# A two-layer trunk: waiting products queued behind dense ones, first slots as whole float32 products, rotary tables later

## The chip, the cores and the metric

One core of a Trainium2 chip runs the whole kernel in one launch. The metric is device microseconds (us) of one execution: the median of three runs is 1169.4 us, the runs lie between 1166.58 and 1169.9 us.

## The reference

```python
for l in range(2):
    shift, scale, gate = split(silu(c) @ ada_w[l] + ada_b[l])
    h = rms_norm(x, norm_pre[l]) * (1 + scale) + shift
    p = h @ w_in[l]                       # all branches' inputs, 1024 wide
    o_mla  = attention(...) ; o_rwkv = rwkv7(...) ; o_gla = gla(...)
    merged = sigmoid(gate_a) * o_mla + sigmoid(gate_b) * o_rwkv + sigmoid(gate_c) * o_gla
    x = x + gate * rms_norm(merged @ w_out[l], norm_post[l])
```

There are 256 tokens (T) of 1024 channels (D) in float32. The attention branch (MLA) compresses queries and keys, turns a part of them by a rotary table of cosines and sines of the positions, and attends in causal blocks. The RWKV-7 branch has 16 heads and a recurrent state with a delta rule. The gated linear attention (GLA) has 4 heads.

## The kernel before

Activations stand with channels on the 128 partitions and the 256 tokens along the free axis. Weights come in slots of 256 columns: two chunks of 512 KB, loaded through the SP queue into a ring of four buffers `wr` (`weights`, L336). For each chunk ScalarE (ACT) casts a rounded part `hi` (L347), and VectorE (DVE) or GpSimd (POOL) subtracts it to get the rest `lo` (L348). `split` (L385) cuts the activations in the same way into `hhi` and `hlo`. A dense slot is `dense_pair` (L376): for each of two output blocks and eight depth blocks three fp32r products, hi by hi, hi by lo and lo by hi, 48 of 128x256 in all, issued by `dense` (L360) or, token-major, by `dense_tok` (L369).

The program goes through each layer like this: a prenorm with the lora slot, the GLA gates (`gla_gates`), `rw_prep` and `rw_chain` for the first half of the RWKV heads, `gla`, then `rw_prep` and `rw_chain` for the second half, `mla` with the RWKV output as filler, and `finish`. For layer 0 the prenorm is `start` (L271): it loads the input transposed (`xn`, 1 MB), takes the norm through `sums`, `rms_row`, `to_rows` and `spread`, and works six slots (lora, two rk, two rr, one rv) depth block by depth block, since the modulation of each depth block comes from two 512 KB chunks of `ada_w` (`ada_part`, L257; DVE multiplies and accumulates each at L266).

`rw_chain` (L556) first forms Gram matrices, sends the small triangular systems through DRAM (tiles `bd`, `Bb`), solves them on POOL in 31 steps of a multiplication `tm` (L601) and an addition to `Xb` (L604), and sends the result through DRAM (`xd`, `Xs`) to the place where TensorE wants it. Eight state steps follow, each with products `z`, `u` (which reads `Xs`, L686), `sp` and `y` on TensorE and copies on DVE and ACT between. There are four such solves: two in each layer. `rope_tables` (L175) makes the rotary tables on POOL in some 34 instructions of 128x256, with two sines on ACT, ahead of `start`.

No instruction order is written out by hand. The tile framework's scheduler lays the whole program out from its own costs and from the order in which the code is written; each engine (TensorE is PE here) then runs its own list in order and waits for semaphores. An instruction that waits holds everything behind it on its engine.

Of the kernel before, what the change touches and what calls it, by code (L numbers as in the profile page):

```python
# [20 lines left out]
P = 128  # L21
T = 256
# [54 lines left out]
def trunk(  # L77
# [97 lines left out]
    def rope_tables():  # L175
        with tc.tile_pool(name="rope", bufs=1, reuse_waits="tile") as rp:
# [8 lines left out]
            def wrap(t):  # L185
                r = rp.tile([P, T], F32, tag="wrap", name="wrap", bufs=2)
                G.tensor_scalar(r, t, MAGIC, -MAGIC, ALU.add, ALU.add)
                G.tensor_sub(t, t, r)

            first = True  # L190
            for k, hi, lo in pieces:
                m = MAGIC * 2.0 ** k
                n = rp.tile([P, T], F32, tag="n", name="n", bufs=2)
                G.tensor_scalar(n, ang, m, -m, ALU.add, ALU.add)
                G.tensor_sub(ang, ang, n)
                a = rp.tile([P, T], F32, tag="ta", name="ta", bufs=2)
                G.tensor_scalar(a, n, 2.0 ** -k, hi, ALU.mult, ALU.mult)
                wrap(a)
                b = rp.tile([P, T], F32, tag="tb", name="tb", bufs=2)
# [7 lines left out]
            b = rp.tile([P, T], F32, tag="tb", name="tb2", bufs=2)  # L207
# [34 lines left out]

    pending = []
# [13 lines left out]
    def ada_part(L, l, slots, pool=None):  # L257

        for s in slots:
            for i in range(2):  # L260
                if pool is None:
                    w = wts.tile([P, D], F32, tag="wr", name=f"adaw{l}_{s}", bufs=4)
                else:
                    w = pool.tile([P, D], F32, tag="adaw", name=f"adaw{l}_{s}", bufs=6)
# [6 lines left out]
    def start(L, hl, firsts, order):  # L271
# [4 lines left out]
        G.memset(zero, 0.0)  # L276
        xn = pp.tile([P, KD, T], F32, name="xn0")
        nc.sync.dma_start(xn, xt)
# [10 lines left out]
        slots, ks, left = [], [], {}  # L289

        def mm(w, ps, k):
            left[id(ps)] -= 1
            ws = slice(k * P, (k + 1) * P)
            for i, (hi, lo) in enumerate(w):
                for j, (wt, at) in enumerate(((hi, hhi), (hi, hlo), (lo, hhi))):
                    PE.matmul(
                        ps[:, i], wt[:, ws], at[:, k],
                        start=False, stop=i == 1 and j == 2 and left[id(ps)] == 0)

        for what in order:  # L300
            if what == "a":
# [3 lines left out]
                hT = pp.tile([P, T], F32, tag="hT0", name="hT0", bufs=3)  # L305
                A.activation(hT, xn[:, k], AF.Identity, scale=L.s1[:, k:k + 1], bias=L.mod[:, k:k + 1])
                split(hhi[:, k], hlo[:, k], hT)
# [3 lines left out]
            else:  # L311
                n, src, pool, tag = firsts[len(slots)]
                j = len(slots)
                w = weights(src, n, pool=None if j < 2 else pp, sub=G if j in (1, 3, 4, 5) else V)
                ps = pool.tile([P, 2, T], F32, tag=tag, name=f"ps_{n}")
                left[id(ps)] = KD
                early[n] = ps
                PE.matmul(
                    ps.rearrange("p a b -> p (a b)"), zero.broadcast_to([P, P]), zero.broadcast_to([P, 512]),
                    start=True, stop=False)  # L320
                slots.append((w, ps))
                for k in ks:
                    mm(w, ps, k)
# [28 lines left out]
    def dense(ps, w, kt, i, act):  # L352
# [6 lines left out]
        for i, (wt, act, k) in enumerate(seq):  # L359
            PE.matmul(  # L360
                ps, wt[:, at + k * P:at + (k + 1) * P], act(k), start=i == 0, stop=i == len(seq) - 1)

    def dense_tok(ps, w, kt, n, act, st):
# [3 lines left out]
        for i, (j, act, k) in enumerate(seq):  # L367
            wt = w[k * n // CHUNK][j]
            PE.matmul(  # L369
# [87 lines left out]
    def rw_prep(L, l, qp, h, sh):  # L457
# [6 lines left out]
        with tc.tile_pool(name=f"rp{n}", bufs=1, side="right", reuse_waits="tile") as rp:  # L464
            lora = rp.tile([P, 512], F32, name="lora")
            nc.sync.dma_start(lora, w2a2[l, :, qp * 512:(qp + 1) * 512])
# [32 lines left out]
            ssk = ps_m.tile([P, 2, 8], F32, tag="m", name="ssk")  # L499
            for s in range(2):  # L500
                g2 = slice(2 * s, 2 * s + 2)
                ps = dense_pair(win[l, S_RK[qp] + s], f"rk{n}{s}", h)
                kam = rp.tile([P, 2, T], F32, tag="t2", name="kam", bufs=3)
                sq = rp.tile([P, 2, T], F32, tag="t2", name="sq", bufs=3)
                for i in range(2):
# [5 lines left out]
                    sums(ssk[:, :, 2 * g:2 * g + 2], sq[:, i], halfsel)  # L511
                    G.tensor_scalar(kam[:, i], av[:, g], L.p("k_a", j), L.omka(j), ALU.mult, ALU.add)
                V.tensor_mul(ks[:, g2], ks[:, g2], kam)
            rn = rp.tile([P, 2, 8], F32, name="rn")
            A.activation(rn, ssk, AF.Sqrt)
# [778 lines left out]
```

## Time and profile before

| what | before |
|---|---|
| median of three runs | 1169.4 us |
| profiled execution | 1166.57 us, span 1164.8 us |
| PE busy | 1079.6 us, 93% of the span |
| DVE, ACT, POOL busy | 791.8, 577.7, 471.3 us |
| mean granted TensorE clock | 0.958 of full speed |
| DMA, mean over the span | 159 GB/s, 185.15 MB |

The span is the profiled execution itself, the execution's time is about 2 us more. Busy time of PE holds pipelined ends, so 93% does not mean that PE worked at its peak for 93% of the time. What a wait costs is read from the idle time in front of an instruction and from the engine that released it.

### The profile page before, as it was taken

How to read it: one execution, taken by the hardware profiler on the slowest of the kernel's cores; microseconds unless marked ns; L12 is line 12 of the kernel's file. 1: busy time of each engine (PE TensorE's matmuls, PEld its weight loads, DVE VectorE, ACT ScalarE, POOL GpSimd, SP SyncE). 2: the span in 40 equal slices, each digit the busy share in tenths (PEclk: the TensorE clock that was granted, in tenths of full speed). 3: DMA queues.
4: the chain of work that ended last, by engine and by line, in shares of the span. 5: the costliest groups of instructions: out<-in, count | busy, mean ns of one | idle time of the engine just before them, and what ended most of it. 6: DMA issues, size and time to landing. Idle time of an engine off the chain costs nothing.

```text
span 1164.8 us, 25067 instructions
## 1 busy us (share of the span) xinstructions
PE 1079.6 (93%) x10293; PEld 983.8 (84%) x10293; DVE 791.8 (68%) x1204; ACT 577.7 (50%) x982; POOL 471.3 (40%) x618
## 2 busy tenths in 40 slices
PE   5789998899999699999989998899999979999997
PEld 3688888798898588899989888888899968789997
DVE  6968855766887667667665674475578666766773
ACT  4356334446456253446556833264374645446452
POOL 7963538424526833203100635641064754310210
PEclk7799899899999899999999989999999989999999
DMA  9655655555466454446755245434434543244761
GB/s 350 226 192 169 167 149 160 178 182 154 151 219 192 142 163 95 129 140 198 243 178 157 88 145 155 125 93 146 144 120 151 167 130 106 73 128 147 246 221 40
DMA packets 70067, 185.15 MB, mean 159 GB/s; under 512 B 24608, under 2 KB 25120, under 8 KB 69824
## 3 DMA queue, kind: packets, MB, share of 16 engines
q1 hardware_dynamic: 48304, 173.37, 47.6%
q10 hardware_dynamic: 21648, 10.18, 3.4%
q8 instruction: 81, 1.33, 0.5%
q14 instruction: 34, 0.28, 0.1%
HBM read 179.32 MB, written 4.20 MB: 158 GB/s over the span
## 4 chain that ended last, share of the span: by engine, by line
PE 58%; POOL 18%; DMA 9%; DVE 6%; issue 4%; ACT 3%; ACTq 1%; DVEq 0%; SPq 0%; POOLq 0%
PE ps_gt L360 10%; PE ps_wo L360 9%; POOL tm L601 6%; POOL Xb L604 6%; PE ps_rz L360 4%; PE y L369 3%; PE ps_rv L360 2%; PE ps_gq L360 2%; PE ps_gv L369 2%; PE ps_mz L360 2%; PE ps_cq L360 2%; DMA wr_wout<-in_wout_dram 2%; DMA Bb<-bd 1%; PE sp L696 1%; DMA Xs<-xd 1%
## 5 line engine op out<-in xcount | busy, mean ns | idle before, releaser
L360 PE MATMUL ps_gt<-hhi,lo_gt 128*128 128x256 f32 x384 | 107.9, 281 | 0.0
L360 PE MATMUL ps_gt<-hhi,hi_gt 128*128 128x256 f32 x384 | 107.9, 281 | 0.0
L360 PE MATMUL ps_gt<-hlo,hi_gt 128*128 128x256 f32 x384 | 107.4, 280 | 0.0
L348 DVE TENSOR_TENSOR lo_gt<-wr_gt,hi_gt 128x1024 fp32r<-128x1024 f32 x48 | 61.7, 1288 | 41.2 <-ACT hi_gt L347 41.1
L348 DVE TENSOR_TENSOR lo_wo<-wr_wo,hi_wo 128x1024 fp32r<-128x1024 f32 x48 | 67.4, 1403 | 31.2 <-ACT hi_wo L347 31.0
L266 DVE SCALAR_TENSOR_TENSOR adaw<-adaw,cb 128x1024 f32<-128x1024 f32 x48 | 68.8, 1437 | 25.5 <-DMA adaw<-in_ada_dram 25.3
L601 POOL TENSOR_TENSOR tm<-Xb,Bb 128x126 f32<-128x126 f32 (+22 forms) x124 | 65.0, 524 | 32.7 <-DMA Bb<-bd 18.2
L347 ACT CAST hi_gt<-wr_gt 128x1024 fp32r<-128x1024 f32 x48 | 50.4, 1050 | 52.8 <-PE ps_gt L360 19.3
L360 PEld LDWEIGHTS ps_gt<-hhi,lo_gt 128*128 128x128 f32 x384 | 72.3, 188 | 0.8
L360 PEld LDWEIGHTS ps_gt<-hlo,hi_gt 128*128 128x128 f32 x384 | 72.5, 189 | 0.5
L360 PEld LDWEIGHTS ps_gt<-hhi,hi_gt 128*128 128x128 f32 x384 | 72.2, 188 | 0.6 <-issue 0.2
L347 ACT CAST hi_wo<-wr_wo 128x1024 fp32r<-128x1024 f32 x48 | 50.5, 1051 | 44.4 <-PE ps_wo L360 21.4
L779 POOL TENSOR_TENSOR merged<-merged,tg 128x512 f32<-128x512 f32 x14 | 25.6, 1827 | 113.1 <-DVE tg L778 90.0
L604 POOL TENSOR_TENSOR Xb<-Xb,tm 128x126 f32<-128x126 f32 (+22 forms) x124 | 63.2, 510 | 9.1
L706 POOL TENSOR_TENSOR gst<-ST,GC 64x256 f32<-64x256 f32 x48 | 34.9, 727 | 74.9 <-DVE ST L710 63.2
L637 POOL COPY bks<-vs 128x128 f32<-128x128 f32 x32 | 14.1, 439 | 115.0 <-PE ptok L644 102.6
L648 ACT COPY vals<-ptok 32x128 f32<-32x128 f32 x128 | 32.9, 257 | 47.1 <-PE ptok L644 32.2
L690 DVE COPY vals<-u 32x128 f32<-32x128 f32 x128 | 36.5, 286 | 9.0 <-PE u L686 7.3
L369 PE MATMUL ps_gv<-hi_gv,hhi 128*128 128x256 f32 x128 | 38.5, 305 | 3.3 <-ACT hi_gv L347 2.2
L1031 POOL TENSOR_SCALAR pr<-pr,sm 128x128 f32<-128x128 f32 (+1 forms) x32 | 28.1, 892 | 27.9 <-DVE sm L1029 27.6
L369 PE MATMUL ps_gv<-hi_gv,hlo 128*128 128x256 f32 x128 | 38.4, 302 | 0.9 <-DVE hlo L389 0.9
L360 PE MATMUL ps_wo<-glo,hi_wo 128*128 128x256 f32 x128 | 36.7, 287 | 2.1 <-DVE glo L389 2.1
(501 smaller groups left out, 4321.5 us busy)
## 6 DMA issues: line engine op xcount, KB each, us to landing
adaw<-in_ada_dram SPq DMA_DIRECT2D x48, 512.0 KB, 4.5
wr_gt<-in_win_dram SPq DMA_DIRECT2D x48, 512.0 KB, 3.9
wr_wo<-in_wo_dram SPq DMA_DIRECT2D x48, 512.0 KB, 4.3
wr_rk<-in_win_dram SPq DMA_DIRECT2D x16, 512.0 KB, 4.6
wr_rr<-in_win_dram SPq DMA_DIRECT2D x16, 512.0 KB, 4.7
wr_rv<-in_win_dram SPq DMA_DIRECT2D x16, 512.0 KB, 3.9
wr_gv<-in_win_dram SPq DMA_DIRECT2D x16, 512.0 KB, 4.6
wr_gz<-in_win_dram SPq DMA_DIRECT2D x16, 512.0 KB, 4.9
```

Of the source, the lines that this page charges most:

```text
L266: V.scalar_tensor_tensor(w, w, 0.5, cb, ALU.mult, ALU.mult, accum_out=L.mod[:, ADA_ORDER[2 * s + i]:ADA_ORDER[2 * s + i] + 1],)
L347: A.copy(hi, wr)
L348: (sub or V).tensor_sub(lo, wr, hi.bitcast(F32))
L360: PE.matmul(ps, wt[:, at + k * P:at + (k + 1) * P], act(k), start=i == 0, stop=i == len(seq) - 1)
L369: PE.matmul(ps, act(k)[:, st * P:(st + 1) * P], wt[:, k * n % CHUNK:k * n % CHUNK + n], start=i == 0, stop=i == len(seq) - 1,)
L601: G.tensor_mul(tv, Xb[:, 0:nr, m:m + 1].broadcast_to([P, nr, w]), Bb[:, m:m + 1, m + 1:32].broadcast_to([P, nr, w]))
L604: G.tensor_add(Xb[:, 0:nr, m + 1:32], Xb[:, 0:nr, m + 1:32], tv)
L648: A.copy(vals[ch % 2][rows(g2, 1 - gh), :, gh, g2], pt[32 * g:32 * g + 32, 2].rearrange("p (q v) -> p q v", q=2))
L690: V.tensor_copy(val[rows(g2, gh), :, gh, g2], u[rows(g2, gh)])
L706: G.tensor_mul(gst[chan(qi)], ST[chan(qi), :, qi], R.GC[chan(qi), :, ch:ch + 1].broadcast_to([64, 4, 64]))
L779: (V if b == 2 and s == 3 else G).tensor_add(m, m, tg)
L1031: G.tensor_scalar(pr[:, ks], pr[:, ks], sm[:, 4 + qt:5 + qt], None, ALU.mult)
```

## The change

1. `start`: the first six slots are whole float32 products from weights that the DMA puts straight into 8 KB tiles, without `hi` and `lo`; 96 float32 products 128x256 stand for 288 fp32r ones. The norm is taken with a matrix of ones (eight float32 products, a square root on ACT, a reciprocal of 128x256 on DVE). The modulated `xn` overwrites itself, and `split` into `hhi` and `hlo` comes after. The sequence of loads (`W` a weight slot, `a` an `ada_w` pair) changes.
2. `rope_tables` is called behind the first `gla`; its tiles have one buffer in place of two.
3. `behind()` puts the instructions issued under it behind the last dense product: the sums of `rw_prep` (`ssk`, `bonp`), the sums of `gla` (`gss`) and its transposes `pk`, and the eight state steps of `rw_chain`, which now come back as a function `steps` and run inside `project` of `gla` or inside `mla`.
4. The loads of `lora` and `gw2` go from the SP queue to the ACT queue.
5. `gla`: ACT takes the results of gq and gk out of PSUM, DVE then multiplies from SBUF; the additions `gsq` (and `csq` in `mla`) go from POOL to DVE; the first `gz` slot stands ahead of the last sum.
6. `mla`: `rotate` copies PSUM to SBUF by ACT and multiplies from there; the shared key's rotation `kr` moves to the front.

```diff
+    last = [None]
+    def behind():
+        return tc.issue_after(last[0].ins)
...
-        ss = ps_m.tile([P, 2, KD], F32, tag="m", name="ss0")
+        ss = ps_m.tile([P, T], F32, tag="m", name="ss0")
...
-                sums(ss[:, :, 2 * s + i:2 * s + i + 1], sq[:, i], one_b)
-        ri = rms_row(pp, ss, 1.0 / D, "0")
+                PE.matmul(ss, ones, sq[:, i], start=s + i == 0, stop=s + i == 4)
+        A.activation(ri, ss, AF.Sqrt, scale=1.0 / D, bias=eps6)
+        V.reciprocal(ri, ri)
...
-            for i, (hi, lo) in enumerate(w):
-                for j, (wt, at) in enumerate(((hi, hhi), (hi, hlo), (lo, hhi))):
-                    PE.matmul(
-                        ps[:, i], wt[:, ws], at[:, k],
-                        start=False, stop=i == 1 and j == 2 and left[id(ps)] == 0)
+            for i in range(2):
+                last[0] = PE.matmul(
+                    ps[:, i], w[:, i, k * P:(k + 1) * P], xn[:, k],
+                    start=False, stop=i == 1 and k == KD - 1)
...
-                w = weights(src, n, pool=None if j < 2 else pp, sub=G if j in (1, 3, 4, 5) else V)
+                w = pp.tile([P, 2, CHUNK], F32, name=f"w_{n}")
+                for i in range(2):
+                    nc.sync.dma_start(w[:, i], src[:, i * CHUNK:(i + 1) * CHUNK])
...
+            def pair_sums(ps, src, s):
+                with behind():
+                    for i in range(2):
+                        g = 2 * s + i
+                        sums(ps[:, :, 2 * g:2 * g + 2], src[:, i], halfsel)
...
             po = dense_pair(wo[l, b, s], f"wo{l}{b}{s}", oh)
+            if ("wo", s) in hooks:
+                with behind():
+                    hooks["wo", s]()
...
-            V.scalar_tensor_tensor(qd[:, g2], ps, GLA_SCALE, e1[:, g2], ALU.mult, ALU.mult)
+            A.activation(qd[:, g2], ps, AF.Copy, scale=GLA_SCALE)
+            V.tensor_mul(qd[:, g2], qd[:, g2], e1[:, g2])
...
-            G.tensor_add(sq[:, 0], sq[:, 0], sq[:, 1])
-            sums(ss[:, :, hd:hd + 1], sq[:, 0], one_b)
+            V.tensor_add(sq[:, 0], sq[:, 0], sq[:, 1])
+        zss = [silu2(gp, win[l, S_GZ], f"gz{l}0", h, "g2", 3)]
+        row_sums(3)
...
-        project(gp, l, 0, S_GATE_C, h, oh, merged, "g2", 3)
+        project(gp, l, 0, S_GATE_C, h, oh, merged, "g2", 3, hooks={("wo" if l == 0 else "gate", 0): steps})
...
-                V.tensor_mul(b[dst], ps[src], sinT[src].unsqueeze(1).broadcast_to([32, 2, T]))
+                V.tensor_mul(b[dst], a[src], sinT[src].unsqueeze(1).broadcast_to([32, 2, T]))
...
-        rope_tables()
...
-        ), "WaWaWaWaWaWaaa")
+        ), "aWaWaWaWaWaWaa")
...
-            gla(L, l, h, gates, merged, gp)
+            gla(L, l, h, gates, merged, gp, steps)
             glap.close()
+            if l == 0:
+                rope_tables()
```

PE at the first slots of `start`, the kernel before (three fp32r products a depth block, with `hhi`, `hlo` and the two parts of the weights):

```order
L296 MATMUL ps_lora_227<-hhi_100,hi_lora_215 128x256
L296 MATMUL ps_rk_260<-hhi_100,hi_rk_248 128x256
L296 MATMUL ps_lora_227<-hlo_101,hi_lora_215 128x256
L296 MATMUL ps_lora_227<-hhi_100,lo_lora_216 128x256
L296 MATMUL ps_lora_227<-hhi_100,hi_lora_221 128x256
L296 MATMUL ps_lora_227<-hlo_101,hi_lora_221 128x256
L296 MATMUL ps_lora_227<-hhi_100,lo_lora_222 128x256
L296 MATMUL ps_rk_260<-hlo_101,hi_rk_248 128x256
```

The same place on PE in the change (`xn` is the modulated input, `w_` a weight as it came):

```order
L302 MATMUL ss_127<-sq_140,ones 128x256 x2
L313 MATMUL ps_lora_115<-xn_112,w_lora_161 128x256 x2
L313 MATMUL ps_rk_117<-xn_112,w_rk_178 128x256 x2
L313 MATMUL ps_lora_115<-xn_112,w_lora_161 128x256 x2
L313 MATMUL ps_rk_117<-xn_112,w_rk_178 128x256 x2
L313 MATMUL ps_rk_119<-xn_112,w_rk_199 128x256 x4
```

The products no longer read `hi`, `lo`, `hhi` or `hlo`, and two stand where six stood.

POOL at the start of the first solve, the kernel before (`bks` scales the keys, `tm` and `Xb` are the solve):

```order
L637 COPY bks<-vs_744 128x128
L640 TENSOR_TENSOR bks<-BK_746,GC_747 128x256
L886 TENSOR_TENSOR gsq<-gsq 128x256
L594 MEMSET Xb 128x512
L596 MEMSET Xb 64x16 x2
L601 TENSOR_TENSOR tm<-Xb,Bb 128x31
L604 TENSOR_TENSOR Xb<-Xb,tm 128x31
L601 TENSOR_TENSOR tm<-Xb,Bb 128x30
L604 TENSOR_TENSOR Xb<-Xb,tm 128x30
```

The same place on POOL in the change (L180 to L216 are `rope_tables`: `ang`, `n`, `ta`, `tb`, `turn` and `wrap` are its tiles, L628 and L631 the solve):

```order
L197 TENSOR_SCALAR ta<-n 128x256
L628 TENSOR_TENSOR tm<-Xb,Bb 128x31
L187 TENSOR_SCALAR wrap<-ta 128x256
L194 TENSOR_SCALAR n<-ang 128x256
L631 TENSOR_TENSOR Xb<-Xb,tm 128x31
L188 TENSOR_TENSOR ta<-ta,wrap 128x256
L195 TENSOR_TENSOR ang<-ang,n 128x256
L628 TENSOR_TENSOR tm<-Xb,Bb 128x30
L201 TENSOR_TENSOR ta<-ta,tb 128x256
L631 TENSOR_TENSOR Xb<-Xb,tm 128x30
```

The rotary tables, which stood ahead of everything, now stand between the last GLA gates and the eighth solve step, and 20 of their instructions stand between solve steps.

PE at the first `u` of layer 1, the kernel before (`ps_gz` is the first output slot of GLA, `gss` a sum of GLA):

```order
L360 MATMUL ps_gz_9287<-hhi_7098,hi_gz_9281 128x256
L360 MATMUL ps_gz_9287<-hlo_7099,hi_gz_9281 128x256
L360 MATMUL ps_gz_9287<-hhi_7098,lo_gz_9282 128x256
L686 MATMUL u<-zs,Xs 32x64 x8
L638 MATMUL ptok<-cs,bks 128x128
L644 MATMUL ptok<-cs,bks 128x128 x2
L146 MATMUL gss<-cs,gsq 128x1 x2
```

The same on PE in the change (`ps_gt` and `ps_wo` are slots of `project`, which follows all of GLA's heads):

```order
L373 MATMUL ps_gt_9428<-hhi_6836,lo_gt_9417 128x256
L373 MATMUL ps_wo_9366<-glo_8485,hi_wo_9354 128x256
L373 MATMUL ps_wo_9366<-ghi_8483,lo_wo_9355 128x256
L716 MATMUL u<-zs,Xs 32x64 x8
L665 MATMUL ptok<-cs,bks 128x128
L671 MATMUL ptok<-cs,bks 128x128 x2
L373 MATMUL ps_wo_9366<-ghi_8483,hi_wo_9354 128x256
```

The first product that needs the solve has moved from the first `gz` slot to the first output slot of `project`. Counted in dense products of 128x256 between the last Gram matrix and the first `u`, the four chains of the program have 359, 356, 295 and 355 before and 474, 346, 515 and 337 in the change.

## Rows read from the trace of the kernel before

**Rows 1.** The page: the span, and part 1.

```profile
span 1164.8 us, 25067 instructions
PE 1079.6 (93%) x10293; PEld 983.8 (84%) x10293; DVE 791.8 (68%) x1204; ACT 577.7 (50%) x982; POOL 471.3 (40%) x618
```

**Rows 2.** What PE waited for: us in total, times, longest.

```profile
PE u L686 <- DMA Xs<-xd: 13.4, 3, 8.1
PE ps_uk L360 <- DVE rotb L923: 6.9, 1, 6.9
...
PE gss L146 <- POOL gsq L886: 5.5, 3, 3.5
PE pk L859 <- POOL far L840: 3.8, 1, 3.8
...
PE ssk L146 <- ACT sq L510: 2.3, 2, 1.8
PE ps_gk L360 <- DVE qd L827: 2.3, 1, 2.3
...
PE pg L794 <- DMA gw<-in_gw_dram: 2.2, 1, 2.2
```

**Rows 3.** Stretches: us, then busy us by engine, granted clock, DMA share, GB/s.

```profile
20.00:40.00 20.00, 11.81 (x41) 8.76 (x42) 19.43 (x27) 6.06 (x9) 19.69 (x16) 0.51 0.93 342
40.00:60.00 20.00, 15.26 (x113) 14.64 (x112) 17.36 (x24) 7.34 (x11) 19.52 (x13) 0.91 0.50 159
...
80.00:160.00 80.00, 72.63 (x621) 65.90 (x619) 63.78 (x88) 41.80 (x66) 35.19 (x32) 0.91 0.57 162
...
640.00:780.00 140.00, 128.03 (x1181) 118.89 (x1181) 83.81 (x119) 68.60 (x108) 71.34 (x114) 0.93 0.41 119
```

**Rows 4.** Timeline of PE in the first 90 us: start, us, instruction.

```profile
1.45 2.08 PE L318 MATMUL ps_lora<-zero 128*128 128x512 f32 x2 [1.45 <-POOL zero L276]
...
6.01 1.89 PE L318 MATMUL ps_rr<-zero 128*128 128x512 f32 x4
...
22.38 0.58 PE L296 MATMUL ps_lora<-hhi,hi_lora 128*128 128x256 f32 x1
...
61.76 0.28 PE L296 MATMUL ps_rr<-hhi,hi_rr 128*128 128x256 f32 x1
...
65.15 0.28 PE L296 MATMUL ps_rr<-hhi,lo_rr 128*128 128x256 f32 x1
...
77.77 0.28 PE L296 MATMUL ps_rv<-hhi,lo_rv 128*128 128x256 f32 x1
```

**Rows 5.** Timeline of DVE in the same stretch.

```profile
28.35 3.38 DVE L266 SCALAR_TENSOR_TENSOR adaw<-adaw,cb 128x1024 f32<-128x1024 f32 x1
...
35.21 1.21 DVE L266 SCALAR_TENSOR_TENSOR adaw<-adaw,cb 128x1024 f32<-128x1024 f32 x1
```

**Rows 6.** Groups of POOL in the first 80 us: largest and smallest of `rope_tables`.

```profile
L188 POOL TENSOR_TENSOR ta<-ta,wrap 128x256 f32<-128x256 f32 x3 | 4.6, 1524 | 0.2
...
L203 POOL COPY turn<-ta 128x256 f32<-128x256 f32 x1 | 0.4, 403 | 0.0
```

**Rows 7.** Timeline of POOL around the first solve.

```profile
160.99 0.29 POOL L637 COPY bks<-vs 128x128 f32<-128x128 f32 x1 [10.89 <-PE ptok L644]
...
172.58 0.24 POOL L601 TENSOR_TENSOR tm<-Xb,Bb 128x31 f32<-128x31 f32 x1 [5.46 <-DVE lo_gz L348]
...
186.19 0.74 POOL L886 TENSOR_TENSOR gsq<-gsq 128x256 f32<-128x256 f32 x1
...
187.42 0.41 POOL L601 TENSOR_TENSOR tm<-Xb,Bb 128x126 f32<-128x126 f32 x1
187.91 1.29 POOL L604 TENSOR_TENSOR Xb<-Xb,tm 128x126 f32<-128x126 f32 x1
...
214.09 0.68 POOL L604 TENSOR_TENSOR Xb<-Xb,tm 128x16 f32<-128x16 f32 x1
```

**Rows 8.** Timeline of PE at the first `u`.

```profile
224.14 0.65 PE L686 MATMUL u<-zs,Xs 32*32 32x64 f32 x16 [2.65 <-DMA Xs<-xd]
```

More of the change, by code (lines that the diff above doesn't have):

```diff
@@ L311, in start @@
             else:
-                n, src, pool, tag = firsts[len(slots)]
-                j = len(slots)
-                w = weights(src, n, pool=None if j < 2 else pp, sub=G if j in (1, 3, 4, 5) else V)
[L315 to L321, printed above, removed]
+                n, src = firsts[len(slots)][:2]
+                w = pp.tile([P, 2, CHUNK], F32, name=f"w_{n}")
+                for i in range(2):
+                    nc.sync.dma_start(w[:, i], src[:, i * CHUNK:(i + 1) * CHUNK])
+                early[n] = banks[len(slots)]
+                slots.append((w, early[n]))
                 for k in ks:
-                    mm(w, ps, k)
+                    mm(*slots[-1], k)
+        for k in range(KD):
+            split(hhi[:, k], hlo[:, k], xn[:, k])
     def ada_in(L, k0=0, k1=8):
@@ L711, in rw_chain @@
-            y = ps_c.tile([P, 2, 64], F32, tag="c", name="y")
-            of_state(y, 1)
-            for qi in range(2):
-                for g2, gh in pairs:
-                    of_chunk(y, 1, chan(g2), g2, gh, qi)
-            A.copy(Y[:, ch], y)
-            if not last:
-                ST = STn
-        mean = rc.tile([P, 16], F32, name="mean")
-        var = rc.tile([P, 16], F32, name="var")
-        Yh = Y.rearrange("p c q v -> p (c q) v")
-        V.tensor_reduce(mean, Yh, AX.X, ALU.add)
@@ new lines, in steps @@
+                y = ps_c.tile([P, 2, 64], F32, tag="c", name="y")
+                of_state(y, 1)
+                for qi in range(2):
+                    for g2, gh in pairs:
+                        of_chunk(y, 1, chan(g2), g2, gh, qi)
+                A.copy(Y[:, ch], y)
+                if not last:
+                    ST = STn
+            mean = rc.tile([P, 16], F32, name="mean")
+            var = rc.tile([P, 16], F32, name="var")
+            Yh = Y.rearrange("p c q v -> p (c q) v")
+            V.tensor_reduce(mean, Yh, AX.X, ALU.add)
@@ L752, in silu2 @@
+            for s in range(2):
+                bc = ps_c.tile([P, 2, T], F32, tag="c", name="bc2")
+                for i in range(2):
+                    spread2(bc[:, i], R.bon, 2 * (2 * s + i))
+                bv = rc.tile([P, 2, T], F32, tag="vb", name="bv", bufs=2)
+                V.tensor_mul(bv, R.vs[:, 2 * s:2 * s + 2], bc)
+                o = orw[:, qp * 4 + 2 * s:qp * 4 + 2 * s + 2]
+                G.tensor_add(o, o, bv)
+        return steps
     def silu2(pool, src, name, h, tag, bufs=2):
@@ L855, in gla, with row_sums @@
             A.copy(at[0:64, st, :, 64:128], px)
-        kt = gp.tile([P, 4, P], F32, name="kt")
-        pk = ps_m.tile([P, 4, P], F32, tag="m", name="pk")
-        for hd in range(4):
-            PE.transpose(pk[:, hd], ks[:, hd], ident)
-        A.copy(kt, pk)
         og = [big(f"og{i}") for i in range(2)]
         ss = ps_m.tile([P, 2, 4], F32, tag="m", name="gss")
+        sqs = []
+        def row_sums(hd):
+            with behind():
+                sums(ss[:, :, hd:hd + 1], sqs[hd][:, 0], one_b)
         for hd in range(4):
@@ L872, in gla @@
                 A.copy(v, ps)
+            if hd == 0:
+                with behind():
+                    kt = gp.tile([P, 4, P], F32, name="kt")
+                    pk = ps_m.tile([P, 4, P], F32, tag="m", name="pk")
+                    for i in range(4):
+                        PE.transpose(pk[:, i], ks[:, i], ident)
+                    A.copy(kt, pk)
+            else:
+                row_sums(hd - 1)
             kv = ps_m.tile([P, T], F32, tag="m", name="kv")
@@ L1000, in mla @@
                 keys_values(n)
+            with behind():
+                steps()
             for s in range(4):
```

260 lines of the change are left out of this document (138 added, 122 removed).

## Prediction

> **What bounds the kernel now.** I read the page first: PE is busy for 1079.6 of 1164.8 us [rows 1]. So most of the time can only go with PE work, and a reordering can win no more than what PE idles or runs at a low clock. The table of what PE waited for [rows 2] shows where it idles: for the result of the RWKV solves (`u`, 13.4 us in three places), for the rotation in front of `ps_uk` (6.9), for POOL's sum `gsq` (5.5), and in single places for `pk`, `ssk`, `ps_gk` and `pg` (2 to 4 each). Then I read the stretches [rows 3]: the start is far from full. Between 20 and 40 us PE is busy for 11.8 of 20 us at a granted clock of 0.51, while DVE and POOL are busy for nearly all of it and the DMA engines too (0.93); from 40 to 60 us DVE is still busy for 17.4 and POOL for 19.5, and the DMA share falls to 0.50. The start waits for loads first and for cutting weights after that. Around later idle spots the clock is 0.91 (80 to 160 us) and 0.93 (640 to 780 us), where other stretches stand at 1.00, so an idle spot costs more than its own length.
>
> **The change part by part.** All sums are made against the profiled execution, 1166.57 us; the median of the runs is 2.8 us above it.
>
> *The start.* Removed: 288 fp32r products. From 61.76 to 65.15 us 29 of them follow each other [rows 4], 0.117 us each, so 33.7 us in all. Added: 96 float32 products of 128x256. The zeroing product of 128x512 is float32, and two take 1.89 us with their tail at 6.01 us [rows 4]; their four passes lie 0.43 us apart, so one of 256 columns costs 0.43 us, and 96 cost 41 us. PE thus gets 8 us more to do. What goes are 12 casts on ACT, 12 subtractions on DVE and POOL, and the rotary work of POOL beside them; the multiplication of an `ada_w` chunk took 3.38 us where it collided and 1.21 us where it did not [rows 5], so DVE should come to 16 times 1.21 plus small pieces, well under 40 us. What is left is the loading: up to the second chunk of the eighth `ada_w` pair the SP queue now has 35 transfers of 512 KB, 18.4 MB, and at 342 GB/s [rows 3] that is 54 us. After it come two multiplications (2.4 us), small pieces (about 1 us) and twelve products (5.2 us): 63 us, and I put 65. The last early product started at 77.77 us [rows 4]. That is 13 us; 2 I take off, since DVE must finish two further `ada_w` chunks before it frees the banks of these slots. **Start: 11 us won.** Ends: 17, if the clock is high and nothing queues; 0, if the products run at 0.58 us on average, between the two levels of the clock (22.38 us, where the first one starts in [rows 4], plus 56). The norm by a matrix of ones takes 8 products of 0.43 us in place of sums and two small transposes: I count nothing, since the first weights and `ada_w` chunks are still arriving; without that cover it is 3 us. Its reciprocal of 128x256 has no row; it lies between 0.4 us (a copy of that size on POOL, [rows 6]) and 3.4 us [rows 5] and beside loads as well.
>
> *GLA gates and queries, 80 to 160 us.* ACT now empties the banks of gq, so the wait of `ps_gk` for `qd`, 2.3 us [rows 2], should go, and about 1 us of clock with it (0.91, [rows 3]). **3 us won**, ends 0 and 6. The loads of `gw2` and `lora` leave the SP queue; PE waited 2.2 us for the former [rows 2], and I leave that wait in place, because on the ACT queue it stands behind the eviction of the lora slot. The Trainium skill (Trainium Kernel Development and Optimization, Key Constraints) says that DMAs issued from SP, ACT and POOL share the same 16 engines and a second issuing engine saves issue time alone; by that rule the wait stays as I have it, and without the rule one would count up to 2.2 us more.
>
> *The first solve.* 20 rotary instructions now stand between its first eight steps. In this solve 10 of 62 instructions collided with DVE: the same size took 0.41 and 1.29 us [rows 7]. Half of the 20 read one tile (0.40 us, the smallest in [rows 6]) and half two (0.74 us, as `gsq` in [rows 7]); a sixth of them collided at 0.9 us more: 14 us. Four `gsq` additions of 0.74 us leave POOL. The solve so ends 11 us later than its start gives. PE has 115 more dense products ahead of the first `u` (474 for 359), 13.4 us, but no longer the stall of 3.5 us for `gsq` [rows 2]. The stall of 2.65 us [rows 8] becomes 2.65 + 11.3 - 13.4 + 3.5 = 4 us. 3.5 won, 1.4 lost: **2 us won**. Ends: 6 with 0.4 us for every rotary instruction, and 13 lost with 1.52 us [rows 6]. The other 14 rotary instructions I cost at nothing: POOL idles 10.89 us ahead of 160.99 us and again up to 172.58 us, when the blocks arrive [rows 7].
>
> *The second solve of layer 0.* The dense products ahead of `u` are 346 for 356, and the additions of the rotation, which `ps_uk` waited for [rows 2], still stand behind the solve's 18th step. **Nothing**, ends 5 won (copies by ACT free the banks) and 4 lost (the state steps now stand behind keys and values).
>
> *Layer 1, 640 to 720 us.* The sums `ssk` and their transposes move behind dense products: 1.8 us [rows 2] and about as much again, and some clock (0.93 over 640 to 780 us, [rows 3]). **5 us won**, ends 2 and 7.
>
> *First solve of layer 1.* 515 dense products for 295 ahead of `u`, 25 us more cover: the 2.6 us there, a third place in the 13.4 [rows 2], go, as do 1.8 of the 5.5 for `gsq` and about half of 3.8 for `pk`, which is still behind the solve on POOL. With a little clock: **7 us won**, ends 3 and 11.
>
> *Second solve of layer 1.* 337 for 355 dense products: the largest stall, 8.1 us [rows 2], stays. **Nothing**, ends 3 either way.
>
> Sum: 11 + 3 + 2 + 0 + 5 + 7 + 0 = 28 us; 1166.6 - 28 = 1138.6, and with the 2.8 us to the median **1141.4 us**.
>
> **The rivals.**
>
> *The orders hold, but the waits only change their names (partial).* Gates 0, layer 1 2 + 3, start 11, first solve -2: 14 won, 1155.4 us. For it: ACT, already a releaser, gets more copies in its queue; against it: it is busy for half of the time [rows 1].
>
> *The rotary tables hold up the first solve.* If all 34 fall behind the arrival of the blocks at the prices of the start (the 19 groups of that stretch sum to 38.4 us, of which [rows 6] shows the largest and the smallest), the solve ends 35 us later, the stall is 28 us, the stage loses 22 in place of winning 2: 4 won in all, 1165.4 us. For it: the two sines stand in ACT's queue between products' squares, and POOL waits for one of them; against it: POOL's idle time ahead of the solve. A rule of the Trainium skill speaks for it (GPSIMD Engine Reference, Key points): POOL shares its way into SBUF with DVE, which blocks it with two-input instructions, and the change makes more of these; the pairs of 0.41 and 1.29 us agree with it.
>
> *The float32 products run at the low clock (slower).* PE idles at the start as loads arrive, and 0.51 was granted there [rows 3]. At the lower level one product takes 0.86 us, 96 take 83 us, and the slots end at 105 us, 27 later than before: 28 - 11 - 27 = 10 lost, 1179.4 us. It decides the sign from an average of 0.72 us a product, when the slots end at about 92 us. For it: the zeroing product at 1.45 us took 2.08 us [rows 4]. Against it: with fewer cuts to wait for, PE is nearly always busy from the third slot on, and the clock rose to 0.91 with PE busy for 15 of 20 us [rows 3].
>
> *Everything is covered (better).* The upper ends together would give 55 us; with half of what lies between, 1128 to 1119 us. For it: the seven waits in [rows 2] alone sum to 36 us, and the low clock around them comes on top; against it: two of four solves keep their cover.
>
> **How the numbers follow.** Chances: the forecast 0.45, partial 0.20, rotary tables 0.14, low clock 0.09, better 0.12. The median and its measurement can tell 0.3% from no change, 3.5 us: faster is below 1165.9 us, slower above 1172.9. Faster: 0.45 + 0.12 + 0.18 of the partial case + 0.05 of the rotary one = 0.80; same: 0.02 + 0.05 = 0.07; slower: 0.09 + 0.04 = 0.13. The range leaves out the low clock and the far end of the better case and of the rotary one: 1119 to 1168 us; the forecast's own is 1128 to 1154.
>
> **What would show it.** Right: the last float32 product near 65 us, at 0.43 us each; `ps_gk`, `gss` and `ssk` gone from what PE waited for; one wait for `Xs` of about 4 us in layer 0, none in the first solve of layer 1, some 8 us in the second. Wrong: float32 products at 0.86 us, a stall of 15 us or more at the first `u`, or new waits of PE for ACT's copies that sum to over 10 us.

## The result and the profile after

The changed kernel takes 1176.72 us (median of four runs, 1174.82 to 1178.51) beside 1169.37 us for the kernel before (median of four): a ratio of 1.0067, with a 95% interval of 1.0045 to 1.009. In the mean it is slower by 7.9 us (5.3 to 10.5), where 1141.4 us were forecast and 1119 to 1168 was the range. The profiled execution took 1177.02 us, its span is 1175.2 us at a mean granted clock of 0.955.

The page of the changed kernel, as in [rows 1]:

```profile
span 1175.2 us, 24799 instructions
PE 1086.4 (92%) x10176; PEld 988.3 (84%) x10176; DVE 768.8 (65%) x1211; ACT 570.9 (49%) x980; POOL 442.1 (38%) x597
```

PE is busy for 7 us more, as 96 float32 products for 288 fp32r ones should make it. DVE, ACT and POOL all have less to do. So the loss is in waits. What PE waited for in the changed kernel (us in total, times, longest), beside [rows 2]:

```profile
PE sc L1071 <- POOL qr L981: 19.8, 2, 10.3
PE u L716 <- DMA Xs<-xd: 11.7, 3, 8.1
PE ps_lora L313 <- ACT xn L322: 8.3, 2, 6.7
PE gss L146 <- DVE gsq L939: 7.1, 2, 4.3
PE pk L921 <- POOL far L882: 4.5, 1, 4.5
...
PE gram L595 <- DVE bv L777: 2.3, 1, 2.3
```

The wait of `ps_uk` is gone, and so is the longest one for `u`, which stood in the second chain of layer 1; the 8.1 us for `u` here stand in the first chain of layer 0. A new wait is the largest: the attention scores `sc` wait twice for `qr`, the addition that ends the rotation of the queries, which stands on POOL between solve steps. `gss` waits longer than before, though its addition has left POOL. The stretches of the changed kernel (as in [rows 3]):

```profile
0.00:20.00 20.00, 11.97 (x28) 6.15 (x28) 9.17 (x16) 7.67 (x11) 2.78 (x14) 0.94 0.91 339
20.00:40.00 20.00, 19.91 (x82) 16.98 (x83) 11.23 (x31) 4.19 (x9) 0.00 (x0) 0.89 1.03 408
40.00:60.00 20.00, 18.40 (x85) 15.88 (x85) 16.10 (x33) 6.94 (x12) 2.38 (x4) 1.00 0.87 332
...
200.00:240.00 40.00, 28.81 (x275) 26.70 (x274) 25.30 (x32) 13.81 (x21) 19.96 (x31) 0.87 0.60 183
240.00:360.00 120.00, 114.79 (x1288) 102.14 (x1287) 90.91 (x160) 63.30 (x121) 41.73 (x48) 0.95 0.52 165
360.00:480.00 120.00, 107.13 (x945) 92.52 (x944) 77.50 (x153) 51.07 (x109) 65.78 (x100) 0.91 0.45 135
```

The last three of these stretches in the kernel before:

```profile
200.00:240.00 40.00, 35.08 (x334) 32.52 (x333) 28.31 (x41) 17.72 (x30) 19.56 (x32) 0.91 0.60 182
240.00:360.00 120.00, 118.45 (x1395) 106.15 (x1394) 90.77 (x150) 61.40 (x119) 46.81 (x53) 1.00 0.56 173
360.00:480.00 120.00, 107.30 (x972) 90.56 (x975) 84.96 (x170) 56.45 (x115) 65.61 (x99) 0.96 0.51 149
```

The start works as meant: the loads run at 332 to 408 GB/s through the first 60 us, PE is nearly always busy from 20 us on, and the clock is up. From 200 to 360 us PE is busy for 10 us less than before, and from 200 to 480 us the granted clock is lower by 0.04 to 0.05.

Two readings of the timeline of PE tell where. The first is PE's idle time (pieces of 0.25 us and more, in us) between places that both programs pass:

| stretch | before | change |
|---|---|---|
| to the first GLA query product `ps_gq` (86.9 us; change 72.6) | 23.1 | 9.7 |
| from there to layer 0's first `ps_rz` (427.5; 425.8) | 28.1 | 37.0 |
| from there to layer 1's `ps_lora` (625.5; 632.0) | 4.5 | 7.3 |
| from there to layer 1's first `ps_rz` (991.8; 992.9) | 21.4 | 23.6 |
| from there to the end | 0.9 | 4.1 |
| sum | 78.0 | 81.7 |

The start idles for 13 us less, everything behind it for 17 us more, and the float32 products add 8 us of work (41.3 for 33.7). That makes 11 to 12 us, beside 10.4 us of span. The second reading is when the Gram matrices of the four chains begin, since each opens a solve: at 149.9, 345.8, 692.8 and 891.9 us before and at 131.2, 350.8, 697.4 and 905.9 us in the change. The first comes 18.7 us earlier, the second is already 5.0 us late though the dense `ps_cq` just ahead of it (324.3 and 313.5 us) is 10.8 us early, and the fourth is 14 us late. The fourth on the timeline of PE, before and in the change, and the wait that follows it in the change:

```profile
891.86 0.34 PE L568 MATMUL gram<-AR,BK 64*64 64x64 f32 x8
...
905.86 1.32 PE L595 MATMUL gram<-AR,BK 64*64 64x64 f32 x64
...
960.06 0.80 PE L1071 MATMUL sc<-kr,qr 64*128 64x128 f32 x4 [10.26 <-POOL qr L981]
```

The first solve itself, on POOL's timeline of the changed kernel (L628 and L631 are the solve, L187 to L216 the rotary tables):

```profile
153.15 1.09 POOL L628 TENSOR_TENSOR tm<-Xb,Bb 128x31 f32<-128x31 f32 x1
154.21 2.06 POOL L187 TENSOR_SCALAR wrap<-ta 128x256 f32<-128x256 f32 x1
156.23 1.35 POOL L194 TENSOR_SCALAR n<-ang 128x256 f32<-128x256 f32 x1
157.55 0.25 POOL L631 TENSOR_TENSOR Xb<-Xb,tm 128x31 f32<-128x31 f32 x1
...
180.47 0.73 POOL L188 TENSOR_TENSOR t<-t,wrap 128x256 f32<-128x256 f32 x1
181.16 1.37 POOL L631 TENSOR_TENSOR Xb<-Xb,tm 128x96 f32<-128x96 f32 x1
...
218.55 0.23 POOL L631 TENSOR_TENSOR Xb<-Xb,tm 128x16 f32<-128x16 f32 x1
```

It lasts 65.6 us, from 153.15 to 218.8; before, it lasted 42.2 us, from 172.58 on [rows 7]. Between its steps 20 rotary instructions take 21.4 us, 1.07 us each. The rest of the difference is small: the 62 solve instructions themselves take 35.2 us for 32.3, and four GLA multiplications `og` between them 6.5 us, where three `gsq` and three `og` took 6.1. The tables reach ACT too, on whose timeline the sine stands between two squares of GLA:

```profile
164.87 0.60 ACT L937 ACTIVATE gsq<-po 128x512 f32<-128x512 f32 x1 [1.82 <-PE po L934]
165.48 1.28 ACT L211 ACT_TABLE_LOAD   x1
174.68 0.42 ACT L211 ACTIVATE sinT<-turn 128x256 f32<-128x256 f32 x1 [7.91 <-POOL turn L188]
175.00 1.03 ACT L360 CAST hi_gz<-wr_gz 128x1024 fp32r<-128x1024 f32 x1
175.93 0.59 ACT L937 ACTIVATE gsq<-po 128x512 f32<-128x512 f32 x1
```

ACT stood still for 7.9 us for the tables with the last square behind it. On PE that is the longer wait for `gss`, and the longer solve is the longer wait at the first `u` (timeline of PE, changed kernel; 2.65 us in [rows 8]):

```profile
178.36 0.98 PE L146 MATMUL gss<-cs,gsq 128*128 128x1 f32 x4 [4.33 <-DVE gsq L939]
...
227.28 0.65 PE L716 MATMUL u<-zs,Xs 32*32 32x64 f32 x16 [8.15 <-DMA Xs<-xd]
```

### The profile page after: what moved, and what is told of

Its sections match the earlier page's. It is cut to its first block, busy times and chain, and to the rows that moved or that the text cites. A ratio compares the mean times of both kernels' runs of the same rounds, so it can differ in the third digit from the quotient of the medians.

```text
span 1175.2 us, 24799 instructions
## 1 busy us (share of the span) xinstructions
PE 1086.4 (92%) x10176; PEld 988.3 (84%) x10176; DVE 768.8 (65%) x1211; ACT 570.9 (49%) x980; POOL 442.1 (38%) x597
## 4 chain that ended last, share of the span: by engine, by line
PE 55%; POOL 16%; DMA 13%; DVE 8%; issue 4%; ACT 3%; ACTq 1%; SPq 0%; DVEq 0%; POOLq 0%
PE ps_gt L373 9%; PE ps_wo L373 9%; POOL tm L628 6%; POOL Xb L631 5%; PE ps_rz L373 4%; PE y L382 4%; PE ps_rv L373 3%; PE ps_rk L373 3%; DMA wr_wout<-in_wout_dram 2%; DMA adaw<-in_ada_dram 1%; PE ps_cq L373 1%; PE ps_gq L373 1%; PE ps_rr L373 1%; DMA Bb<-bd 1%; PE sp L726 1%
## 5 line engine op out<-in xcount | busy, mean ns | idle before, releaser
L272 DVE SCALAR_TENSOR_TENSOR adaw<-adaw,cb 128x1024 f32<-128x1024 f32 x48 | 60.9, 1273 | 34.5 <-DMA adaw<-in_ada_dram 34.3
L628 POOL TENSOR_TENSOR tm<-Xb,Bb 128x126 f32<-128x126 f32 (+22 forms) x124 | 70.6, 569 | 31.9 <-DMA Bb<-bd 23.2
L631 POOL TENSOR_TENSOR Xb<-Xb,tm 128x126 f32<-128x126 f32 (+22 forms) x124 | 65.4, 527 | 8.9
L382 PE MATMUL y<-hi_wout,m2hi 128*128 128x256 f32 x128 | 37.4, 298 | 4.3 <-ACT m2hi L404 4.3
L373 PE MATMUL ps_wo<-ghi,hi_wo 128*128 128x256 f32 x128 | 37.2, 290 | 2.4 <-ACT ghi L401 2.3
L382 PE MATMUL y<-hi_wout,m2lo 128*128 128x256 f32 x128 | 38.0, 299 | 1.3 <-DVE m2lo L405 1.3
```

The lines of the kernel that those rows point to most:

```text
L272: V.scalar_tensor_tensor(w, w, 0.5, cb, ALU.mult, ALU.mult, accum_out=L.mod[:, ADA_ORDER[2 * s + i]:ADA_ORDER[2 * s + i] + 1],)
L373: last[0] = PE.matmul(ps, wt[:, at + k * P:at + (k + 1) * P], act(k), start=i == 0, stop=i == len(seq) - 1)
L382: last[0] = PE.matmul(ps, act(k)[:, st * P:(st + 1) * P], wt[:, k * n % CHUNK:k * n % CHUNK + n], start=i == 0, stop=i == len(seq) - 1,)
L628: G.tensor_mul(tv, Xb[:, 0:nr, m:m + 1].broadcast_to([P, nr, w]), Bb[:, m:m + 1, m + 1:32].broadcast_to([P, nr, w]))
L631: G.tensor_add(Xb[:, 0:nr, m + 1:32], Xb[:, 0:nr, m + 1:32], tv)
```

## The experiments

Each kernel ran beside the kernel before on the same chip (three chips in all). Results are ratios to the kernel before, with 95% intervals; 0.001 is 1.2 us. A difference between two of these ratios is uncertain by some 4 to 5 us. Theory A puts the loss on the rotary tables inside the first solve, theory B on the state steps behind the output projection, theory C on the addition `qr` on POOL.

**Rotary tables ahead of the start again.**

```diff
+        rope_tables()
         start(L, hl, (
...
-            if l == 0:
-                rope_tables()
```

> The change with the rotary tables built ahead of the first slots again, all else as in the change. Theory A (the 20 rotary instructions between the steps of the first solve, some 21 us there, put off the state steps, the Gram matrices of the second chain and with them the second solve): the first solve shortens from 65.6 to about 45 us, the wait of 8.15 us for the first u and the 4.3 us for gss go, the wait of 9.6 us for the first rotated queries shrinks to under 4, and the time falls by 12 to 20 us to 1157 to 1165. Rival B (the order of the state steps decides, the rotary tables only fill time that is waited out anyway): the solve shortens as well, but the second chain's Gram matrices stay where they are and the time falls by less than 4 us, 1173 to 1177. POOL's work at the start is no longer hidden by subtractions there, so both expect the start to stay within 2 us.

Measured: 1.0002 (0.9968 to 1.0036), against 1.0067 of the change: 7.6 us won, between the figures of theory A and rival B. The first solve lasts 38.1 us instead of 65.6, and the first `u` comes at 218 us for 227. The tables do cost time there, but less than theory A said: PE's wait of 9 us for `qr` in each layer stayed, and a new wait of 9.3 us appeared in front of `gbc`, of which more below. The start did not stay within 2 us, as expected: `ps_gq` comes at 76.1 us for 72.6. So the tables cost 3.5 us at the start; from there to layer 1's `ps_lora` this kernel takes 547.1 us for 559.4, which is 12.3 us won.

**State steps right behind each solve again.**

```diff
             steps = rw_chain(L, l, 0, R, orw, rc)
+            steps()
+            steps = lambda: None
```

and the same for the second chain.

> The change with the eight state steps of every chain issued where they stood before, right behind the solve, all else as in the change. Theory B (steps that wait behind the output projection put off the next chain's Gram matrices, by some 14 us in layer 1): the second chain of layer 1 starts 10 us or more earlier, the wait of 10.3 us for the last rotated queries goes, a wait for the solve's result of some 2 to 8 us comes back in the first chain of layer 1, and the time falls by 5 to 12 us to 1165 to 1172. Theory A: the rotary tables still hold up layer 0, so layer 0 gains at most 3 us, and in layer 1 the gain of the first chain (12 us) is given back; the time stays within 4 us of 1176.7.

Measured: 0.9996 (0.997 to 1.0021): 8.3 us won. That is theory B; theory A had expected nothing here. In layer 1 the second chain's Gram matrices come at 886 us in place of 906, and the wait for `qr` there has gone (9.0 us in one place are left of 19.8 in two). The second chain of layer 0 stays late (its Gram matrices at 348.9 us).

**Both.**

> Both of the above: rotary tables ahead of the first slots, and state steps issued right behind the solve. Theory A: the time is that with the rotary tables moved alone, within 4 us. Theory B: it is 8 us or more below it, since the next chain no longer waits. If both hold and add, 1150 to 1158.

Measured: 0.995 (0.9926 to 0.9975). From 1.0067 that is 13.7 us, beside 7.6 and 8.3 alone: within the intervals the two causes add. In this kernel the timeline of ACT shows where the new wait at `gbc` comes from:

```profile
180.54 0.60 ACT L788 ACTIVATE tz<-ps_gz 128x512 f32<-128x512 f32 x1
191.41 0.34 ACTq L633 DMA_DIRECT2D xd<-Xb  x1
191.84 1.04 ACT L360 CAST hi_gt<-wr_gt 128x1024 fp32r<-128x1024 f32 x1 [10.70 <-POOL Xb L631]
```

The transfer of the solve's result is issued by ACT, which stands 10.7 us for the solve's end with casts of weights and the row `rowsg` of the GLA norm behind it.

**The new start alone**, on the kernel before:

```diff
-        ), "WaWaWaWaWaWaaa")
+        ), "aWaWaWaWaWaWaa")
```

with the new `start` and eight `ada_w` buffers, nothing else.

> The kernel before with the new start alone (first six slots as whole float32 products, norm by a matrix of ones, two more buffers for ada_w), nothing else of the change. If the 14 us that the change is ahead at the first GLA query product come from the start and stay: 1154 to 1160. If they are lost to the solves, which POOL sets, whatever follows (rival: a solve's end does not move with PE): 1163 to 1169.

Measured: 0.9937 (0.9908 to 0.9967), 7.4 us won, between the two figures expected. That is half of the 14 us by which the change is ahead at `ps_gq`. In the profile of this kernel `ps_gq` comes at 80.2 us, not at 72.6: PE idles for 13.5 us up to there, not 9.7 (2.4 of them for `gw2`), and the rotary tables still lie on POOL beside it. So the other half is not the start's alone: with the tables first in the whole change `ps_gq` comes at 76.1 us, so some 4 us are the rest of the change, the load of `gw2` among it, and 3.5 us the place of the tables. Behind the start, all that is left of the change (0.995, tables first and steps early, for 0.9937) adds 1.5 us, within the intervals nothing. Start -7.4, this rest +1.5 and the two causes together +13.7 make the 7.8 us of the change by construction, each being the step from one of these kernels to the next.

**The addition `qr` on DVE**, in the change:

```diff
-                G.tensor_add(r, a, b)
+                V.tensor_add(r, a, b)
```

> The change with one edit: the addition that ends the rotation of the queries goes from POOL, where it stands behind the 18th and 25th step of a solve, to DVE. Theory C (the two waits of attention scores for this addition, 19.8 us in the change, are the cost): the waits go and the time falls by 12 us or more, to under 0.997 of the kernel before. Rival A (the solve itself is late, so that PE then waits for its result instead): the waits for the addition go, but waits of 8 us and more for u come in the second chain of each layer, and the time falls by less than 5 us, to 1.002 to 1.007 of the kernel before.

Measured: 1.0073 (1.0047 to 1.0099), nothing won, though the largest wait of the profile is gone. Theory C, that this wait is the cost, falls. What PE waits for in this kernel:

```profile
PE pT L1092 <- POOL pr L1089: 13.8, 1, 13.8
PE ps_mz L373 <- ACT kn L1045: 9.4, 1, 9.4
...
PE u L716 <- DMA Xs<-xd: 8.3, 3, 6.6
```

The next piece of the attention that POOL does, the scaling of the weights `pr`, now stands behind the second solve of layer 0 (the solve ends at 412.9 us, the first `pr` starts at 417.0), and PE waits there until 417.6. It was not at `u`, as rival A had it, but the bound is the one it named: the solve's end.

**The same edit without the two causes** (tables first, steps early):

> Rotary tables ahead of the first slots, state steps right behind the solve (0.995 of the kernel before), and the addition of the rotation on DVE. Theory C: the wait of 11.6 us for the rotated queries in layer 0 goes and 8 to 11 us are won, 0.986 to 0.988. Theory A (the solve of the second chain decides): the wait moves to u, and less than 4 us are won, 0.992 to 0.995.

Measured: 0.9913 (0.9885 to 0.9942), 4.3 us better than 0.995 and between the two figures expected; the intervals overlap. The wait moved to `u` in the second chain of layer 0, in one place of 13.0 us, as theory A had it:

```profile
PE u L716 <- DMA Xs<-xd: 13.0, 1, 13.0
PE gbc L164 <- ACT rowsg L159: 9.2, 1, 9.2
```

**The same edit on the kernel before with the new start:**

> The kernel before with the new start alone (0.9937 of the kernel before) and the addition of the rotation on DVE. Here the wait is of the product ps_uk for the rotation's buffers, 6.5 us, as in the kernel before. Theory C: it goes and 5 to 6 us are won, 0.988 to 0.989. Theory A: it comes back at u, and less than 2 us are won, 0.992 to 0.994.

Measured: 0.9975 (0.9941 to 1.0008), so nothing won over 0.9937; the wait at `ps_uk` became one of 13.0 us of `ps_uv` for ACT, and not one for `u`. Theory A's figure is nearer.

**The solve's result issued by POOL**, with tables first and steps early:

```diff
-        nc.scalar.dma_start(
+        nc.gpsimd.dma_start(
```

at `xd` and at both halves of `Xs`.

> Rotary tables ahead of the first slots and state steps right behind the solve (0.995 of the kernel before), and the two transfers of the solve's result issued by POOL, which ends the solve, in place of ACT. If the 10.7 us that ACT stood at this issue with casts of weights behind it, and the 8.6 us that PE then waited for the GLA norm, are paid for in full: 8 us less, 0.988. If they are hidden behind the wait for the result that comes next anyway: within 3 us of 0.995. The waits for gbc and for casts behind the solve must go in both cases.

Measured: 1.0 (0.9979 to 1.0022), 6 us worse than with ACT. `gbc` no longer waits, but `u` does:

```profile
PE u L716 <- DMA Xs<-xd: 33.2, 4, 12.6
PE sc L1071 <- POOL qr L981: 10.7, 1, 10.7
```

PE got to the first state steps earlier (190.3 us for 199.9) and waited there for more than it had saved. The first and the fourth solve last 41.8 and 42.1 us here, for 37.9 and 35.9 with ACT. Why they are longer, and with it why the time became worse and not equal, stays open.

**Sums of `rw_prep` behind dense products**, on the kernel before with the new start:

```diff
+            def pair_sums(ps, src, s):
...
+                with behind():
+                    for i in range(2):
+                        g = 2 * s + i
+                        sums(ps[:, :, 2 * g:2 * g + 2], src[:, i], halfsel)
...
+                if s:
+                    pair_sums(ssk, sq, 0)
...
-                    sums(ssk[:, :, 2 * g:2 * g + 2], sq[:, i], halfsel)
```

> The kernel before with the new start (0.9937 of the kernel before) and the sums of rw_prep (ssk, bonp) queued behind later dense products, nothing else of the change. If that reordering pays what the prediction gave it (some 5 us in layer 1 and a share of the gates'): 0.987 to 0.990. If the waits of PE for ssk and the transposes are only renamed, or the solve behind them sets the time: within 2 us of the start alone, 0.992 to 0.996.

Measured: 0.9967 (0.9936 to 0.9998) beside 0.9937 without it: no gain. `ssk` still waits, 4.2 us in three places (4.7 in three without the edit).

**Late steps in one chain at a time**, tables first, all others early. In layer 1's first chain:

```diff
+            if l == 0:
+                steps()
+                steps = lambda: None
```

> Rotary tables ahead of the first slots; the state steps of the first chain of layer 1 late, inside the output projection as in the change, those of all other chains right behind the solve (all early: 0.995). Theory B with layer 1 as its place: the wait for u in the first chain goes, the Gram matrices of the second chain come 12 us or more later relative to the dense slots around them, and 4 to 8 us are lost, 0.998 to 1.002. If the loss lies in layer 0: 0.993 to 0.996.

Measured: 0.9992 (0.9974 to 1.0011), 4.9 us lost beside 0.995; the intervals just touch. The timelines of PE show how. With all steps early the second chain's Gram matrices of layer 1 begin at 876.86 us, ahead of the first `ps_cq` (880.21):

```profile
876.86 0.34 PE L595 MATMUL gram<-AR,BK 64*64 64x64 f32 x6
```

With layer 1's late steps they begin 21 us behind the first `ps_cq` (871.90):

```profile
893.14 1.32 PE L595 MATMUL gram<-AR,BK 64*64 64x64 f32 x64
```

The dense work of the compressed queries and keys (`ps_cq` and `ps_ckv`, 871.9 to 892.2 us) is then used up ahead of the Gram matrices; with all steps early it stands behind them (880.2 to 902.7 us), beside the transfers and the start of the solve (898.5 us). And `sc` waits for POOL in both layers (with all steps early in layer 0 alone, 11.6 us):

```profile
PE sc L1071 <- POOL qr L981: 22.1, 2, 11.8
```

In layer 0's first chain (the condition the other way round):

> Rotary tables ahead of the first slots; the state steps of the first chain of layer 0 late, as in the change, all others right behind the solve (all early: 0.995). Theory B with layer 0 as its place: the Gram matrices of the second chain come 6 us or more later and 4 us or more are lost, 0.998 to 1.002. If the loss lies in layer 1, or in the second chains: 0.993 to 0.996.

Measured: 0.9941 (0.9911 to 0.9971): nothing lost, though the Gram matrices of the second chain come 10.0 us later than with all steps early (345.7 us for 335.7), as the expectation of a loss had it. In this layer a late second solve by itself costs nothing that these runs show. In the second chains (`steps` handed to `mla`):

> Rotary tables ahead of the first slots; the state steps of the first chains right behind the solve, those of the second chains behind the keys and values of the attention, as in the change (all early: 0.995). If late steps in the second chains are the part of the 8 us that the late steps of layer 1's first chain (0.9992) leave open: 0.997 to 1.000. If they cost nothing, 0.993 to 0.996, and the rest lay in the late steps and the rotary tables together.

Measured: 0.9922 (0.9897 to 0.9947): nothing lost. So layer 1's first chain is the only one whose late steps lost anything by themselves, 4.9 us. Late steps in all chains lost 6.1 us with the tables first (1.0002 for 0.995) and 8.3 us beside the late tables; the intervals are too wide to settle where the small remainders lie.

**The addition `qr` and the scaling `pr` on DVE**: tables first, steps early, `qr` on DVE as above, and

```diff
-                        G.tensor_scalar(pr[:, ks], pr[:, ks], sm[:, 4 + qt:5 + qt], None, ALU.mult)
+                        V.tensor_scalar(pr[:, ks], pr[:, ks], sm[:, 4 + qt:5 + qt], None, ALU.mult)
```

> Rotary tables ahead of the first slots, state steps right behind the solve, the addition of the rotation on DVE (0.991 of the kernel before), and the scaling of the attention weights also moved from POOL to DVE, so that nothing of the attention stands between solve steps. If attention behind POOL's solve still costs: 3 to 6 us less, 0.986 to 0.989. If only the solve's result is waited for: within 2 us, 0.989 to 0.993, with the wait at u in the second chain of layer 0.

Measured: 0.986 (0.9829 to 0.9891), some 16 us below the kernel before, and the fastest of all. Its page and its longest wait:

```profile
PE 1071.6 (93%) x10176; PEld 976.2 (85%) x10176; DVE 787.5 (69%) x1247; ACT 567.6 (49%) x979; POOL 406.4 (35%) x561
...
PE u L716 <- DMA Xs<-xd: 13.5, 3, 12.0
```

The time is that of the first expectation, the wait, 12.0 us at the first `u` of layer 0's second chain, that of the second. Beside 0.995 the two moves from POOL to DVE pay 10 us. How much of that `pr` pays is not shown: with `qr` alone moved no `pr` stands between steps of the attention's solves any more (in layer 0 the solve ends at 399.6 us, the first `pr` starts at 405.6), the intervals overlap, and the two profiles differ most, by 5 us, between layer 1's `ps_lora` and its second chain's Gram matrices, where there is no attention. Nor is it shown that the early second solve is the condition (352.8 us here, 373.9 in the change, where `qr` alone paid nothing): in the kernel before with the new start that solve begins at 356.3 us, and `qr` alone paid nothing there either. Both moves in the change itself were not run.

## Why the prediction was wrong

**The start** was right in its mechanism: "63 us, and I put 65" for the end of the slots. The last early product and the first dense one behind it in the changed kernel:

```profile
64.79 1.03 PE L313 MATMUL ps_rv<-xn,w_rv 128*128 128x256 f32 x4
65.47 0.47 PE L373 MATMUL ps_rv<-hhi,hi_rv 128*128 128x256 f32 x1
```

The two products at 64.79 us (two records each) take 0.43 us each, as forecast. The slower rival, products at the low clock, is excluded (0.89 to 1.00 granted from 20 to 60 us). The term of 11 us was somewhat too large: 7.4 (3.9 to 10.8), with the rotary tables still beside the start.

**The gates**: 3 us were forecast, and from the first `ps_gq` to the first Gram matrix the change takes 58.6 us for 63.0. The size came out by luck: the new start alone, without any change to the gates, takes 57.8 us there. The wait of `ps_gk` only changed its name (2.3 us for `qd` before, 2.1 for `lo_gk` in the change), as the partial rival had it, and PE idles for 5.6 us in this stretch where it was 4.5. The wait for `gw2` that I left in place is gone: its load was issued at 63.6 us and landed 4.7 us later, ahead of its product at 69.6. The Trainium skill (Trainium Kernel Development and Optimization, Key Constraints) says that a second issuing engine saves issue time alone. The transfer took as long as before (4.7 us, for 4.6 and 5.2), which agrees; but the load is now issued 6.0 us ahead of its product, where it was 4.0 us from SP with the new start alone (70.9 and 74.9 us), and that was enough for PE's wait.

**The first solve**, "2 us won", is the first step that failed, in two places. "14 us" for the 20 rotary instructions: they took 21.4, 1.07 us each. I had priced most of them by the rows of undisturbed instructions, though the 34 of them at the start, 38.4 us, said 1.13. Of the four `gsq` that I took off only three, 2.2 us, had stood inside the solve. And the stall of "4 us" became 8.15, with 7.9 us of ACT standing on the sine on top, a place that I named only within a rival. The Trainium skill's rule (GPSIMD Engine Reference, Key points) that POOL shares its way into SBUF with DVE fits: here the instruction of line L195 took 0.74 and 1.73 us; no run here took DVE away to show that it is the cause. So the rival of the rotary tables had the mechanism, with 20 instructions inside the solve in place of its 34: it put 22 us of loss there, and 7.6 were measured.

**The second solve of layer 0**, "nothing", was an incomplete step: I compared only dense products between a Gram matrix and `u` and did not ask when the Gram matrix itself comes. It came 5.0 us later than before, while the products just ahead were 10.8 us early: it waits for the end of the first chain (2.3 us for `bv`, in what PE waited for above), whose steps waited for the longer solve. The attention's `qr` and four of its `pr` stood between the steps of that solve, and `sc` waited 9.6 us. What this lateness costs by itself is not shown: with the tables first, 10 us of it cost nothing (0.9941 for 0.995).

**Layer 1**: of "7 us won" in the first chain about half was seen. The wait for `u` there is gone, and from the first Gram matrix to `ps_gt` the change takes 75.5 us for 85.6; but part of that is state steps only put off, for with the steps early again it takes 81.9 us (696.1 to 778.0). The 25 us of cover for this solve were taken from what follows. The eight state steps begin at 789 us instead of 756, they last some 85 us from the first `u` to the last as before, and the next chain's Gram matrices come 14 us later. They follow the chain's last `u` by 31.4 us, and by 29.1 in layer 0; before, 50.0 us lay between the two in layer 1. The step "nothing" for the second solve of layer 1 is the one that failed: the change in cover was priced in one chain and its lateness in the next was not. The stall of 8.1 us at `u` that I left in place there became the wait of 10.3 us of `sc` for `qr`, and the late steps lost 8.3 us, 4.9 of them by this chain alone.

**The sums behind dense products**, "5 us won": nothing was measured for those of `rw_prep`. Those of `gla` were not tried apart.

The sum went wrong in a simple way: 28 us were counted as won, and of 78.0 us of idle time on PE the change saved none. What it took away at the start came back behind the solves. By the experiments the 36 us between forecast and measurement come apart roughly like this, each part uncertain by some 4 us: the start 3.6 (11 forecast, 7.4 measured), the first solve with the tables 9.6 (2 won forecast, 7.6 lost), the late steps 15.3 (7 won forecast, 8.3 lost), gates and sums 9.5 (8 won forecast, 1.5 lost), less 2.2 by which the two causes together cost less than one by one. Of the signs of being wrong that I named none came: the float32 products took 0.43 us, the stall at the first `u` is 8 us and not 15, and PE waits for none of the copies that ACT has newly taken over. The wait of `sc` for POOL was not among the signs.

## What to carry to other kernels

Four solves on one engine follow each other through the whole program, and each chain ends in the start of the next. Cover that is moved in front of a wait puts off what stands behind it: ask when the next long item of the slow engine starts, not only how long the wait in hand becomes. Whether that lateness costs time is a question for a run of its own: in layer 1 it cost 4.9 us, in layer 0 nothing. Idle time of a slow engine is the place for extra work only where nothing in line behind it is on such a chain: the rotary tables cost 3.5 us at the start, and 7.6 us more than that inside a solve. The largest line of a table of waits need not be worth anything: removing 19.8 us of waits won nothing while the solve behind them was late, and new waits of 13.8 and 9.4 us took their place.

## What was not expected of the hardware

Float32 products of 128x256 run back to back at 0.43 us (64.79 us above), and 96 of them, loaded whole, were quicker than 288 fp32r products that wait for cuts (0.9937 with the new start alone). From 20 to 40 us PE was busy for 19.91 us where it had been 11.81 [rows 3], and the granted clock was 0.89 where it had been 0.51. A rotary instruction on POOL that reads two tiles of 128x256 took between 0.72 and 1.76 us within one solve.
